# First score tiles in single PSUM banks, an earlier load of head 0, and re-paced weight sums in a two-layer decoder trunk

## The chip, the cores and the metric

The kernel runs on one core of one Trainium2 chip. The metric is the device time of one execution in microseconds; the median of several runs counts. The core has TensorE (PE), VectorE (DVE), ScalarE (ACT), GpSimd (POOL) and SyncE (SP); SP and POOL issue the DMAs here.

## What is computed

The reference is a decoder trunk of two layers on a sequence of 1024 tokens of width 1024, all in float32. Layer 0 is an mLSTM mixer and an MLP; layer 1 is causal attention with eight heads on low-rank keys and values, and an MLP. The hidden width of both MLPs is 4096, and the activation is the square of relu. Cut to what matters here:

```python
def causal_mla_attention(q_nope, q_rope, k_nope, k_rope, v):
    ...
    scale = (B_NOPE + B_ROPE) ** -0.5
    def block(args):
        qn_b, qr_b, start = args
        s = (jnp.einsum('bqhd,bkhd->bhqk', qn_b, k_nope)
             + jnp.einsum('bqhd,bkd->bhqk', qr_b, k_rope)).astype(jnp.float32) * scale
        ...
        s = jnp.where(kpos[None, :] <= qpos[:, None], s, -jnp.inf)
        p = jax.nn.softmax(s, axis=-1)
        return jnp.einsum('bhqk,bkhd->bqhd', p.astype(v.dtype), v)

def sqrelu_mlp(h, w1, w2):
    return jnp.square(jax.nn.relu(h @ w1)) @ w2
```

A query block is 128 tokens; the first one sees 128 keys, the last one 1024.

## The kernel before, in words

**Arithmetic.** Every float32 product is made of three passes with operands split into a high and a low part (`mm3`, L255 to L257): low times high, high times low, high times high. A split is a rounding copy on ACT and a subtraction on DVE (`split_mod`, L531 and L532; for weights L190 and L191, or L549 and L550 where the load and the split are traced apart by `wfetch`).

**Two halves and two streams.** The 1024 tokens are worked in two halves of 512. While one half runs its MLP (the dense stream), the other one's mixer runs in between. `two_streams` does the weaving by hand: the mixer is a generator that yields how many dense steps shall come next, or "align", which lets the dense stream run until its next step is one that makes a hidden tile. The first attention (`attention_first`) is that of tokens 0 to 511 and runs beside layer 0's MLP for tokens 512 to 1023; the second one (`attention_second`), tokens 512 to 1023, runs beside layer 1's MLP for tokens 0 to 511.

**PSUM.** The eight banks are handed out as two single banks `ps`, two single banks `pc` and two pairs of banks `pm`. The MLP makes a hidden tile in `ps` and its second product in `pm`; L199 adds that to the sum in SBUF. Transposes, the rotary product and some projections take `pc`. Attention scores take `pm`.

**One unit of attention.** A unit is one head with two query tiles, number 2j and 2j + 1. `scores` makes both (L1584 to L1590: four passes, on the diagonal block a fifth that adds the mask, and a last one; L1586 and L1587 read the rotary part T of the query) and calls `softmax` for each: maximum on DVE (L1594), scaling of it (L1595), Exp on ACT with the sum (L1596), reciprocal (L1597) and the product (L1598) on DVE, and for the even tile a zeroed block on POOL (L1600). `turned`, in `attend`, transposes the probabilities on PE (L1704) and splits them; `products` multiplies them with the values. For j = 0 one pair of banks holds the two tiles of a head, in one bank each, 128 and 256 keys wide (the matmul writes at least 256 columns). In the first attention the units of two heads go together, with j = 0 and 1; in the second a unit is one head, with j = 2 and 3.

**Preparing.** `prepare_pair` makes keys, values and queries of two heads for the present half. In the second half they go to DRAM (kd, vd, qd, td, 512 KB for each head and kind, td for two heads), and `loaded_head` brings a whole head back, keys and values of both halves: six loads for an even head. `query_rotary` (L1565 to L1570) makes T of the rotated query. All these tiles come from one ring of 24 buffers, `k4`.

**Weight sums.** The last MLP multiplies with sums of blocks of its first weight matrix. `weight_sums` makes them in DRAM with 128 DMAs from POOL, eight for each of 16 groups of rows, some of which add to what is there. Each one is handed out with a small DVE memset (L1046), a POOL copy of it (L1047) and the DMA (L1050 adds, L1052 writes). Of the eight, number 3 to 7 read or add to what the one before or an earlier one wrote. `with_weight_sums` hands out one per step of layer 0's MLP after its first 28 counted steps, and `with_rest` one per step of layer 1's MLP for tokens 0 to 511.

**Order.** The framework orders each engine's instructions before the run, by a priority and a simulated timeline. The priority is the order of tracing; `prompt(f)` traces what `f` makes 300 places ahead. Weight loads, their splits, the splits of hidden tiles and L199 are traced so already.

Of the kernel before, what the change touches and what calls it, by code (L numbers as in the profile page):

```python
# [83 lines left out]
def kernel(  # L84
# [66 lines left out]
    def pc():  # L151
        return pp.tile([P, 512], F32, tag="pc", bufs=2, name=f"pc_{next(uid)}")

    def pm():
        return pp.tile([P, 2, 512], F32, tag="pm", bufs=2, name=f"pm_{next(uid)}")
# [1406 lines left out]
    def query_rotary(qr):  # L1562
        T = k4v(F32R)
        hi = tmp(F32R)
        nc.scalar.copy(hi, qr)  # L1565

        nc.vector.tensor_copy(T[0:64, 0], hi[0:64].bitcast(F32))
        nc.vector.tensor_copy(T[64:128, 1], hi[64:128].bitcast(F32))
        nc.vector.tensor_sub(T[64:128, 0], qr[0:64], hi[0:64].bitcast(F32))
        nc.vector.tensor_sub(T[0:64, 1], qr[64:128], hi[64:128].bitcast(F32))  # L1570
        return T

# [19 lines left out]
    def softmax(f, pr, n, even):  # L1592
        m, l = small(1), small(1)
        nc.vector.reduce_max(m, f, axis=AX.X, negate=True)  # L1594
        nc.vector.tensor_scalar(m, m, SCALE, None, ALU.mult)  # L1595
        nc.scalar.activation(pr[:, :n], f, AF.Exp, bias=m, scale=SCALE, accum_out=l)  # L1596
        nc.vector.reciprocal(l, l)  # L1597
        nc.vector.tensor_scalar(pr[:, :n], pr[:, :n], l, None, ALU.mult)  # L1598
        if even:
            nc.gpsimd.memset(pr[:, n : n + P], 0.0)  # L1600

    def scores(kk, unit):

        (_, q, kn, _), j = unit
        prs = []
        if j < 2:
            st = pm()
            pr = raw().rearrange("p (a b) -> p a b", b=512)
            for e in range(2):
                score_mm(lambda g: st[:, e], kk, q, kn, 2 * j + e)  # L1610
            for e in range(2):
                n = (2 * j + e + 1) * P
                softmax(st[:, e, :n], pr[:, e], n, e == 0)
                prs.append(pr[:, e])
        else:
            for e in range(2):
                st = pm()
                n = (2 * j + e + 1) * P
                score_mm(lambda g: st[:, g], kk, q, kn, 2 * j + e)
                pr = raw()  # L1620
                softmax(st.rearrange("p a b -> p (a b)")[:, :n], pr, n, e == 0)
                prs.append(pr)
        return prs

# [6 lines left out]
    def prepare_pair(p_, hf):  # L1631


        wr, wkv = w_pair_r(p_), w_pair_kv(p_)
        yield 0
        wn, pt = w_pair_n(p_), pc()
        for k in range(3):
            mm3(pt, wr[0][:, k], wr[1][:, k], hf.cq[0][k], hf.cq[1][k], k == 0, k == 2)
        rp = rope(pt, hf)
        next(rp)  # L1640
        kt = [k4v(F32R) for _ in range(2)]
        kn = [(t[:, 0], t[:, 1]) for t in kt]
        k_half(kn, wkv, hf)
        for r in range(2):
            for i in range(2):
                nc.sync.dma_start(kd[2 * p_ + r, i, :, ts(hf.i, H)], kn[r][i].bitcast(F32))
        yield 1
        vt = [k4v(F32R, 256) for _ in range(2)]
        v = v_half(wkv, hf, vt)
        for r in range(2):  # L1650
            for i in range(2):
                nc.sync.dma_start(
                    vd[2 * p_ + r, i, :, ts(hf.i, H)].rearrange("p (t e) -> p t e", e=P),
                    vt[i][:, :, ts(r, P)].bitcast(F32),
                )
        qn = []
        for r in range(2):
            t = k4v(F32R)
            pt = pc() if r else ps()
            for k in range(3):  # L1660
                s = ts(r, P)
                mm3(pt, wn[0][:, k, s], wn[1][:, k, s], hf.cq[0][k], hf.cq[1][k], k == 0, k == 2)
            split_mod(t[:, 0], t[:, 1], pt, None)
            qn.append(t)
        T = query_rotary(last_of(rp))
        if hf.i:
            for r in range(2):
                nc.sync.dma_start(qd[2 * p_ + r], flat(qn[r]))
            nc.sync.dma_start(td[p_], flat(T))
            yield 1  # L1670
        else:
            yield 2
        vs = [[(h_[:, ts(r, P)], l_[:, ts(r, P)]) for h_, l_ in v] for r in range(2)]
        return [(2 * p_ + r, (qn[r], T[:, r]), kn[r], vs[r]) for r in range(2)]
# [18 lines left out]
    def attend(hf, groups, dense, behind=lambda: None):  # L1693


        def turned(work):
            PTh, PTl = hdv(F32R, 256), hdv(F32R, 256)
            n = 0
            for u, b0, nb in work:
                for b in range(b0, b0 + nb, 2):  # L1700
                    pt = pc()
                    for e in range(2):
                        for i in range(2):
                            nc.tensor.transpose(  # L1704
                                pt[:, ts(2 * e + i, P)], u.prs[i][:, ts(b + e, P)], ident
                            )
                    s = slice(n, n + 2)
                    split_mod(PTh[:, s], PTl[:, s], pt.rearrange("p (a b) -> p a b", b=256), None)
                    n += 2
            return PTh, PTl  # L1710

        def products(work, PT):
            n = 0
            for u, b0, nb in work:
                if b0 == 0:
                    u.po = ps()[:, :256]
                for kb in range(b0, b0 + nb):
                    mm3(u.po, *u.v[kb], PT[0][:, n], PT[1][:, n], kb == 0, kb == u.nk - 1)
                    n += 1
                if b0 + nb == u.nk:  # L1720
                    s = ts(u.j % 2, 256)
                    if u.hh < 6:
                        o = tmp()[:, :256]
                        nc.scalar.copy(o, u.po)
                        nc.sync.dma_start(oT[ts(u.hh, P), ts(u.j, 256)], o)
                    else:
                        split_mod(hf.o.hi[u.hh][:, s], hf.o.lo[u.hh][:, s], u.po, None)

        def begin():
            us = []  # L1730
            for head, j in next(groups, []):
                u = Half()
                (u.hh, _, _, u.v), u.j, u.nk = head, j, 2 * j + 2
                u.prs = scores(hf.kk, (head, j))
                us.append(u)
            return us

        late = None
        yield "align"
        us = begin()  # L1740
        yield 1
        while us:
            if sum(u.nk for u in us) <= 4:
                rounds = [[(u, 0, u.nk) for u in us]]
            else:
                rounds = [[(u, b, min(4, u.nk - b))] for u in us for b in range(0, u.nk, 4)]
            for n, work in enumerate(rounds):
                if late:
                    late()
                PT = turned(work)  # L1750
                late = lambda a=(work, PT): products(*a)
                if len(rounds) == 1:
                    yield 1
                if n == len(rounds) - 1:
                    us = begin()
                    if not us:
                        behind()
                yield next(dense)
        late()
# [15 lines left out]
    def attention_second(hf):  # L1775
        pairs = [prepare_pair(p_, hf) for p_ in range(4)]
        next(pairs[0])
        yield 0
        for p_ in range(4):
            if p_ < 3:  # L1780
                yield from primed(pairs[p_], pairs[p_ + 1])
            else:
                yield from pairs[p_]

        def units():
            for hh in range(NH):
                h_ = loaded_head(hh)
                if hh == 6:
                    last_o(hf)
                for j in range(2, 4):  # L1790
                    yield [(h_, j)]

        yield from attend(hf, units(), cycle((1, 0.5, 0.5)), lambda: load_o(hf))
# [365 lines left out]
    steps_done = [0]  # L2159

    def with_weight_sums(g):
        for v in g:
            if v != "within":
                steps_done[0] += 1
                if steps_done[0] > 28:
                    next(wsums, None)
            yield v

# [76 lines left out]
    def with_rest(g):  # L2245

        n = 0
        for v in g:
            if v != "within":
                n += 1  # L2250
                next(wsums, None)
                if n == 61:
                    later[0]()
            yield v
# [53 lines left out]
```

## Time and profile before

| | |
|---|---|
| median of 3 runs | 2362.25 us (2359.37 to 2362.75) |
| the profiled execution's own time | 2359.22 us |
| span in the profile, first to last instruction | 2357.3 us |
| granted clock of TensorE, mean | 0.997 |
| first attention, scores of the first pair to the last | 960.7 to 1199.8 us |
| second attention, first scores to the last | 1566.7 to 1813.1 us |
| DMA, mean rate | 178 GB/s |

In the timeline a row is: start in us, length in us, engine, line of the kernel, operation, the tiles it writes and reads, and the shape. Matmuls are pipelined: a 512-column one is shown with 0.39 us, and the next starts 0.23 us after it. In square brackets stands the idle time of the engine before it and what ended that. A row of the waits is: the waiting engine, tile and line, what it waited for, the total in us, how many times, the longest. A row of a stretch holds its bounds and length, the busy time of PE, PE's weight loads, DVE, ACT and POOL with their counts, the granted clock, the DMA engines' busy share and the rate in GB/s. A row of the chain that ended last is start, length and what it was.

### The profile page before, as it was taken

Reading aid. Unit: us, or ns where it says so; the run is one execution under the profiler, and the core shown is the slowest. Engines: PE = TensorE matmul, PEld = TensorE weight load, DVE = VectorE, ACT = ScalarE, POOL = GpSimd, SP = SyncE. Lnnn points to the kernel's source line nnn. Section 1 sums busy time; section 2 is a strip of 40 time slices with the busy share of each in tenths; the row PEclk is TensorE's granted clock in tenths of the full one; section 3 lists DMA queues with packets and bytes.
Section 4 is the critical chain, followed back from the end, with each engine's and each line's share of the span. In section 5 each row is a group of like instructions: output and inputs, shape, how many; then the busy total and the mean of one; then the engine's idle time right before and its main releaser. Section 6 shows DMA issues by size and latency. Waiting matters only on the chain.

```text
span 2357.3 us, 32527 instructions
## 1 busy us (share of the span) xinstructions
PE 2321.8 (98%) x12181; PEld 1959.9 (83%) x12181; DVE 1605.7 (68%) x2657; ACT 1098.2 (47%) x1826; POOL 155.0 (7%) x353
## 2 busy tenths in 40 slices
PE   7999999999999999999999999999999999999998
PEld 5888898888888888888888888888888888989997
DVE  6677876867685777777764967765656488557556
ACT  4355335654343354334444554434444445655543
POOL 1010000000001110111010110010001000000000
PEclk9999999999999999999999999999999999999999
DMA  9452664545566876667764665885544553656562
GB/s 314 144 153 82 191 184 149 156 141 163 174 184 179 284 222 188 184 195 207 211 160 126 199 200 183 274 274 172 163 134 134 143 164 97 185 173 217 166 185 88
DMA packets 408349, 420.76 MB, mean 178 GB/s; under 512 B 27427, under 2 KB 310112, under 8 KB 404608
## 3 DMA queue, kind: packets, MB, share of 16 engines
q1 hardware_dynamic: 402272, 385.02, 52.1%
q0 software_dynamic: 5920, 33.66, 6.5%
q8 instruction: 96, 1.57, 0.3%
q14 instruction: 61, 0.50, 0.1%
HBM read 359.37 MB, written 92.80 MB: 192 GB/s over the span
## 4 chain that ended last, share of the span: by engine, by line
PE 89%; DVE 5%; DMA 4%; ACT 1%; issue 1%; SPq 0%; DVEq 0%; ACTq 0%
PE ps L255 15%; PE ps L257 15%; PE ps L256 15%; PE pm L255 10%; PE pm L256 10%; PE pm L257 10%; DMA raw<-in_mlp_w_dram 2%; PE pc L256 2%; PE pc L257 2%; PE pc L255 2%; PE pc L1704 1%; DMA raw<-in_a_w_in_dram 1%; PE pm L1590 1%; PE pm L899 1%; PE pm L1584 1%
## 5 line engine op out<-in xcount | busy, mean ns | idle before, releaser
L255 PE MATMUL ps<-k,wl 128*128 128x512 f32 (+1 forms) x1432 | 546.3, 381 | 1.6 <-DVE wl L191 1.3
L257 PE MATMUL ps<-k,wh 128*128 128x512 f32 (+1 forms) x1432 | 539.0, 376 | 0.0
L256 PE MATMUL ps<-k,wh 128*128 128x512 f32 (+1 forms) x1432 | 537.4, 375 | 0.0
L549 ACT CAST wh<-raw 128x1024 fp32r<-128x1024 f32 x272 | 285.0, 1051 | 481.4 <-PE ps L255 149.0
L550 DVE TENSOR_TENSOR wl<-raw,wh 128x1024 fp32r<-128x1024 f32 x272 | 331.7, 1221 | 249.4 <-ACT wh L549 155.4
L255 PEld LDWEIGHTS ps<-k,wl 128*128 128x128 f32 x1432 | 269.6, 188 | 53.7 <-issue 3.6
L257 PEld LDWEIGHTS ps<-k,wh 128*128 128x128 f32 x1432 | 269.4, 188 | 50.1 <-issue 0.7
L256 PEld LDWEIGHTS ps<-k,wh 128*128 128x128 f32 x1432 | 269.8, 188 | 48.9 <-issue 1.7
L199 DVE TENSOR_TENSOR k<-k,pm 128x512 f32<-128x512 f32 (+1 forms) x254 | 210.9, 858 | 83.3 <-PE pm L257 82.0
L191 DVE TENSOR_TENSOR wl<-raw,wh 128x1024 fp32r<-128x1024 f32 (+2 forms) x110 | 128.1, 1166 | 115.6 <-ACT wh L190 115.4
L255 PE MATMUL pm<-hd,wl 128*128 128x512 f32 x512 | 201.4, 393 | 0.5 <-ACT hd L531 0.5
L256 PE MATMUL pm<-hd,wh 128*128 128x512 f32 x512 | 199.3, 390 | 0.2 <-DVE hd L532 0.2
L257 PE MATMUL pm<-hd,wh 128*128 128x512 f32 x512 | 199.3, 390 | 0.0
L255 PE MATMUL pm<-wh,hd 128*128 128x512 f32 x488 | 192.2, 394 | 2.9 <-ACT raw L1596 2.5
L256 PE MATMUL pm<-wl,hd 128*128 128x512 f32 x488 | 190.3, 390 | 0.0
L257 PE MATMUL pm<-wh,hd 128*128 128x512 f32 x488 | 190.2, 390 | 0.0
L190 ACT CAST wh<-raw 128x1024 fp32r<-128x1024 f32 (+2 forms) x110 | 109.4, 996 | 172.3 <-PE ps L255 82.9
L1596 ACT ACTIVATE raw<-pm,sm 128x128 f32<-128x128 f32 (+3 forms) x64 | 47.5, 742 | 152.4 <-DVE sm L1595 122.8
L532 DVE TENSOR_TENSOR hd<-tmp,hd 128x512 fp32r<-128x512 f32 x128 | 88.0, 688 | 38.6 <-ACT hd L531 37.9
L255 PEld LDWEIGHTS pm<-hd,wl 128*128 128x128 f32 x512 | 96.2, 188 | 21.0 <-ACT hd L531 0.9
L256 PEld LDWEIGHTS pm<-hd,wh 128*128 128x128 f32 x512 | 96.2, 188 | 20.5 <-DVE hd L532 0.5
L257 PEld LDWEIGHTS pm<-hd,wh 128*128 128x128 f32 x512 | 96.1, 188 | 20.1
(391 smaller groups left out, 4274.9 us busy)
## 6 DMA issues: line engine op xcount, KB each, us to landing
raw<-in_mlp_w_dram SPq DMA_DIRECT2D x240, 512.0 KB, 4.3
raw<-in_ada_w_dram SPq DMA_DIRECT2D x80, 512.0 KB, 4.6
raw<-in_a_w_in_dram SPq DMA_DIRECT2D x48, 512.0 KB, 4.4
sums<-in_mlp_w_dram POOLq DMA_DIRECT2D x96, 256.0 KB, 4.5
raw<-sums SPq DMA_DIRECT2D x64, 256.0 KB, 3.7
xs<-k SPq DMA_DIRECT2D x40, 256.0 KB, 5.6
raw<-in_kv_ada_w_dram SPq DMA_DIRECT2D x16, 512.0 KB, 4.1
raw<-in_a_w_out_dram SPq DMA_DIRECT2D x16, 512.0 KB, 4.9
```

Source lines behind the costliest of these rows:

```text
L190: nc.scalar.copy(hi[:, :n], r[:, :n])
L191: i = nc.vector.tensor_sub(lo[:, :n], r[:, :n], hi[:, :n].bitcast(F32))
L199: return f(*a, **k)
L255: nc.tensor.matmul(o, ll, rh, start=start, stop=False, **m)
L256: nc.tensor.matmul(o, lh, rl, start=False, stop=False, **m)
L257: pe_last[0] = nc.tensor.matmul(o, lh, rh, start=False, stop=stop, **m)
L532: nc.vector.tensor_sub(lo, u, hi.bitcast(F32))
L549: nc.scalar.copy(hi, u)
L550: nc.vector.tensor_sub(lo, u, hi.bitcast(F32))
L899: nc.tensor.matmul(nv[:, r, i], hf.PT[p_][:, r, cs], v[2 * p_ + r], start=g == 0, stop=True,)
L1584: nc.tensor.matmul(o[:, :w], ql, kh, start=True, stop=False)
L1596: nc.scalar.activation(pr[:, :n], f, AF.Exp, bias=m, scale=SCALE, accum_out=l)
```

## The change

- `scores`: for j = 0 a head's two tiles take one `pc` bank, 256 columns each, where they took a `pm` pair. The j = 1 tiles and the second attention keep `pm`.
- `softmax`, the split of transposed probabilities in `turned`, and `query_rotary` are wrapped in `prompt`.
- `prepare_pair` of the second half loads head 0 (`hf.first`) before it stores the queries and T of the last pair; `units` takes that head in place of loading it itself.
- `with_weight_sums` starts after 44 counted steps, where it started after 28. `with_rest` hands out one operation per step for the first 11 steps, none for steps 12 to 22, and two per step from step 23 on.

```diff
         if j < 2:
-            st = pm()
+            st = pm() if j else pc().rearrange("p (a b) -> p a b", b=256)
             pr = raw().rearrange("p (a b) -> p a b", b=512)
...
                 n = (2 * j + e + 1) * P
-                softmax(st[:, e, :n], pr[:, e], n, e == 0)
+                prompt(softmax)(st[:, e, :n], pr[:, e], n, e == 0)
                 prs.append(pr[:, e])
...
-                softmax(st.rearrange("p a b -> p (a b)")[:, :n], pr, n, e == 0)
+                prompt(softmax)(st.rearrange("p a b -> p (a b)")[:, :n], pr, n, e == 0)
...
-        T = query_rotary(last_of(rp))
+        T = prompt(query_rotary)(last_of(rp))
         if hf.i:
+            if p_ == 3:
+                hf.first = loaded_head(0)
             for r in range(2):
                 nc.sync.dma_start(qd[2 * p_ + r], flat(qn[r]))
             nc.sync.dma_start(td[p_], flat(T))
...
                     s = slice(n, n + 2)
-                    split_mod(PTh[:, s], PTl[:, s], pt.rearrange("p (a b) -> p a b", b=256), None)
+                    prompt(split_mod)(
+                        PTh[:, s], PTl[:, s], pt.rearrange("p (a b) -> p a b", b=256), None
+                    )
...
             for hh in range(NH):
-                h_ = loaded_head(hh)
+                h_ = loaded_head(hh) if hh else hf.first
...
                 steps_done[0] += 1
-                if steps_done[0] > 28:
+                if steps_done[0] > 44:
                     next(wsums, None)
             yield v
...
                 n += 1
-                next(wsums, None)
+                for _ in range(1 if n < 12 else 0 if n < 23 else 2):
+                    next(wsums, None)
                 if n == 61:
                     later[0]()
```

## The prediction

> **What bounds the kernel now.** I read the page first: the share of each engine, then the chain that ended last.
>
> ```profile
> span 2357.3 us, 32527 instructions
> PE 2321.8 (98%) x12181; PEld 1959.9 (83%) x12181; DVE 1605.7 (68%) x2657; ACT 1098.2 (47%) x1826; POOL 155.0 (7%) x353
> PE 89%; DVE 5%; DMA 4%; ACT 1%; issue 1%; SPq 0%; DVEq 0%; ACTq 0%
> ```
>
> PE is busy for 98% of the span and 89% of the chain is its own work. The change leaves PE's work as it is (the same matmuls, to other banks), so all it can win is time that PE waits, and whatever wait goes anywhere moves the end by as much. The next view is therefore PE's waits in the stretches that the diff touches: the first attention (945 to 1220 us), then the second one in two parts.
>
> ```profile
> PE pm L1584 <- DVE k L199: 2.9, 4, 0.9
> PE pm L1584 <- DVE sm L1046: 1.2, 3, 0.5
> PE pm L255 <- ACT raw L1596: 1.9, 2, 1.1
> PE pm L1586 <- DMA k<-td: 1.1, 1, 1.1
> PE pm L255 <- ACT raw L1596: 0.6, 2, 0.4
> PE pc L1704 <- DVE raw L1598: 0.5, 3, 0.2
> ```
>
> The first two rows are the first attention, the next two 1500 to 1620 us, the last two 1620 to 1830 us: 4.1, 3.0 and 1.1 us of idle PE. They understate the loss, because a row ends where a matmul's modelled end lies. The timeline of one place shows by how much, with DVE and ACT beside it:
>
> ```profile
> 960.01 0.39 PE L257 MATMUL pm<-hd,wh 128*128 128x512 f32 x1
> 960.75 0.39 PE L1584 MATMUL pm<-k,k 128*128 128x256 f32 x1 [0.35 <-DVE sm L1046]
> 961.36 0.37 PE L1590 MATMUL pm<-k,k 128*128 128x256 f32 x1
> 961.57 0.27 PE L1584 MATMUL pm<-k,k 128*128 128x256 f32 x1
> 962.07 0.36 PE L1590 MATMUL pm<-k,k 128*128 128x256 f32 x1
> 963.15 0.38 PE L1584 MATMUL pm<-k,k 128*128 128x256 f32 x1 [0.71 <-DVE k L199]
> 970.18 1.03 PE L1704 MATMUL pc<-ident,raw 128*128 128x128 f32 x8
> 958.75 0.69 DVE L1570 TENSOR_TENSOR k<-tmc,tmp 64x512 fp32r<-64x512 f32 x1
> 959.47 1.22 DVE L199 TENSOR_TENSOR k<-k,pm 128x1024 f32<-128x1024 f32 x1
> 961.88 1.21 DVE L199 TENSOR_TENSOR k<-k,pm 128x1024 f32<-128x1024 f32 x1
> 963.68 0.28 DVE L1594 TENSOR_REDUCE sm<-pm 128x1 f32<-128x128 f32 x1
> 964.83 0.40 DVE L1594 TENSOR_REDUCE sm<-pm 128x1 f32<-128x256 f32 x1
> 968.22 0.37 DVE L1598 TENSOR_SCALAR raw<-raw,sm 128x256 f32<-128x256 f32 x1
> 964.26 0.37 ACT L1596 ACTIVATE raw<-pm,sm 128x128 f32<-128x128 f32 x1 [5.31 <-DVE sm L1595]
> ```
>
> The scores of the first head start 0.74 us after the last MLP matmul, where the next 512-column one starts after about 0.23; the second head's start 1.08 after the last of the first, where 961.36 to 961.57 shows 0.21 for the same seam. So 0.51 and 0.87 us are lost where the rows say 0.35 and 0.71: 0.16 more per wait. The reason stands on DVE: both bank pairs (pm) still hold the MLP's products, and the two additions that empty them (L199) end at 960.69 and 963.09, each just before a score starts. (The row that names a memset, L1046, names what lay beside the first of them.)
>
> **Scores in pc banks.** For j = 0 each head takes one 512-column pc bank instead of a pm pair; its two 256-column tiles fit. The four pairs of heads have 7 such waits: 4.1 + 7 x 0.16 = 5.2 us, and up to 6.0 if the slower first matmul behind each wait (about 0.11) goes too. Are the pc banks free? Their last users are the query's evacuation and the rotary product; the latter is read before L1570 can start at 958.75, 1.5 us before the scores are due. What is late next is the rotary query that the third matmul of a score reads: L1570 ends at 959.44, and that matmul would come at about 960.6, so it holds by 1.1 us. After that come the transposes (L1704), which need the softmax. Without the waits (0.51 + 0.87 + 2 x 0.11) the scores end 1.6 us earlier and the transposes are due at 970.18 - 1.6 = 968.6; the softmax of the four tiles on DVE now ends at 968.59 behind the additions. If DVE keeps its order, that is even, with perhaps 0.1 us lost a place; if the softmax, now marked urgent, passes the second addition or the work between the two, nothing. I take 5.2 - 4 x 0.05 = 5.0 us gained; the bounds are 2.0 (each place slips by 0.75) and 6.0.
>
> Sharing a bank has a price of its own: the second tile's maximum may have to wait for the first tile's Exp. In the rows above, in two different banks, it does so already: ACT's Exp ends at 964.63 and the second maximum starts at 964.83. The Trainium skill, PSUM — Partial Sum Buffer, section "PSUM bank collisions raise a hardware error", says that two engines may not touch one bank in the same quadrant at once, reads included, which speaks against this edit. By that rule the first maximum would also wait for the second tile's six matmuls, 0.6 to 0.7 us by their rows, and with four places this part would be 5.0 - 2.6 = 2.4 us. I don't take it, since DVE is busy with the addition until 963.09 anyway, long after those matmuls.
>
> **The early load of head 0.** The second attention's first score waits for the td tile:
>
> ```profile
> 1555.33 3.45 SPq L1668 DMA_DIRECT2D qd<-k  x2
> 1558.83 1.26 SPq L1681 DMA_DIRECT2D k<-kd  x2
> 1566.90 0.39 PE L1585 MATMUL pm<-k,k 128*128 128x512 f32 x1
> 1568.39 0.50 PE L1586 MATMUL pm<-hd,k 128*128 128x512 f32 x1 [1.10 <-DMA k<-td]
> 1560.71 7.64 DMA k<-td
> ```
>
> From 1566.90 to 1568.39 is 1.49 us where 0.23 is due: 1.26 lost. Six loads (two kd, qd, td, two vd) move past two qd stores and one td store on SP's queue; the second qd store keeps SP until 1558.78. Ahead of the stores the loads issue up to 3.5 us earlier, so td lands near 1564.9, 2 us before it is read. The stores come about 6 x 0.4 = 2.5 us later, and only the tiles that they free wait for them. The loads need six k4 tiles while 24 are handed out (8 for the MLP's input, 4 for its sum, 2 + 3 latents, 7 of the last pair); seven of these are done with by then (two stored keys, the latents). I take 1.2 gained, bounds 0 (the loads find no tile and wait) and 1.4.
>
> **Softmax, turned splits and rotary query marked urgent.** No instruction is added; the fixed order on DVE, ACT and POOL changes, and what gets passed is the splits of weights and hidden tiles, which the MLP needs a step or two later. The waits after 1620 us are 1.1 + 5 x 0.27 = 2.4 us (0.16 and 0.11 more for each, as above); most are the length of the softmax itself, which no order shortens. I take 0.3, bounds -0.5 (a late weight split) and 2.4.
>
> **Weight sums.** 128 operations are handed out one per MLP step, and the last starts at 1822.6:
>
> ```profile
> L1046 DVE MEMSET sm<- x128: 59/59/59, 695.5 to 1822.6; 128x1 f32 x128
> 695.00:840.00 145.00, 145.00 (x644) 119.25 (x643) 94.58 (x159) 57.94 (x76) 24.64 (x52) 1.00 0.76 228
> 1500.00:1620.00 120.00, 116.84 (x593) 98.41 (x592) 77.04 (x129) 47.89 (x76) 10.49 (x26) 1.00 0.80 249
> 1620.00:1825.00 205.00, 203.34 (x1155) 174.00 (x1154) 127.80 (x234) 90.29 (x157) 19.84 (x50) 1.00 0.48 147
> q0 software_dynamic: 480, 2.88, 11.6%
> q0 software_dynamic: 736, 4.46, 9.8%
> POOL sums L1050 <- DMA sums<-sums: 26.4, 6, 6.2
> 1974.38 0.92 SPq L236 DMA_DIRECT2D raw<-sums  x2
> ```
>
> By the code 24 + 64 steps hand them out before the second layer, and 40 steps of it the rest; after it is 8 + 64, then 11, none for 11 steps, then 45 in 23 steps: it ends five steps later, near 1855, over 100 us before the first read at 1974.38. Where they go, early on (695 to 840), PE is busy throughout: nothing gained. The 11 silent steps are the stretch from 1500 to 1620, where DMA is at 0.80, of which the sums (q0) are 11.6%. There a weight load takes 8.58 us and is the cause of the two waits in the 1.9 us row above:
>
> ```profile
> 1591.20 8.58 DMA raw<-in_mlp_w_dram
> 1592.63 0.52 POOL L1052 DMA_DIRECT2D sums<-sums  x1
> ```
>
> It lands at 1591.20 + 8.58 = 1599.8, and DVE stands behind its split (L550) with the softmax queued behind that. One 256 KB sum that starts 1.4 us after the load will be gone; the loads of heads beside it stay. Of 1.9 + 2 x 0.27 = 2.4 us I take 1.0, bounds 0 and 2.4.
>
> **The sum.** 5.0 + 1.2 + 0.3 + 1.0 = 7.5 us, by the bounds 1.5 to 12.2. The profiled execution took 2359.22 us (span 2357.3 and 1.9 around it), 3.0 under the median of 2362.25; it would come to 2351.7, and the median to 2354.75, say 2354.8. A measurement of this kernel tells about 0.2%, 4.7 us, from no change.
>
> **Rivals.** (1) Given back: the waits before scores go, but the transposes wait for the softmax (0.75 us at four places) and td or the late load stays: 2.0 + 0.9 = about 3 us, median 2359. For it: DVE's softmax end and the due time of the transposes are even. Against: the urgent mark. (2) Slower: from 1620 on two sums per step make the weight loads late. Behind a late load DVE stands as at 1600, which costs PE 2.4 us each time. Of the 16 units of scores (eight heads, two each) twelve come after 1620; with half of them so struck it is 6 x 2.4 = 14 us against 7.5: median 2369. It decides once DMA there comes near the 0.80 of the stretch that has the late load. The sums (q0) now take 9.8% there; 18 operations become about 35, so the share goes from 0.48 to about 0.58: not near on the mean, though in bursts. By the Trainium skill, DMA: Bandwidth & Descriptors, section "Issuing engines are not separate DMA queues", transfers of POOL and SP run on the same 16 engines and interleave; the two stretches above, 0.80 with a late load and 0.48 with none, agree. POOL's own queue is no cover either: of a step's two operations, one in four pairs reads what its partner writes, and POOL then stands up to 6.2 us, the zeroing for the softmax (L1600) behind it. That gets read about 10 us later, as these rows show, so PE sees none of it unless two such waits follow each other:
>
> ```profile
> 1610.94 0.20 POOL L1600 MEMSET raw<- 128x128 f32 x1 [0.57 <-issue]
> 1621.09 0.60 PE L1704 MATMUL pc<-ident,raw 128*128 128x128 f32 x4
> ```
>
> (3) It doesn't do what it says: the scores keep waiting, now for a pc bank, or the order stays; 0 to 1 us, median 2362.
>
> **How the numbers follow.** Forecast 0.57, (1) 0.24, (3) 0.06, (2) 0.13. Only the forecast is faster by over 0.2%; (1) and (3) are within it, less a little that turns slower by a reshuffled order: faster 0.57, same 0.29, slower 0.14. The low end is the sum of upper bounds with a microsecond for the median's scatter, 2362.25 - 12.2 - 1 = 2349; the high end takes in (1) and (3) and the scatter of the three runs, 2363.5, and leaves (2) out.
>
> **What would show it.** Right: no wait of L1584 on L199 in the first attention; L1584 writes pc there 16 times; L1704 waits under 1 us there; no wait on td; no sums DMA between about 1500 and 1620 and twice the count after it; PE's idle time about 5 us less. Wrong: L1704 waiting on L1598 or POOL for over 3 us; waits of L255 on L1596 growing after 1620 with weight loads that take over 8 us; a wait of the scores for pc.

## The result and the profile after

The changed kernel takes 2374.67 us (median of 5 runs, 2373.26 to 2378.23), the kernel before, run beside it, 2362.25 (5 runs, 2358.35 to 2363.58). The ratio is 1.0057 [1.0043, 1.0070], 13.5 us slower (10.2 to 16.5), where 7.5 us faster was forecast. The profiled execution took 2375.45 us, 16.2 more than that of before. From here on "expected" and "measured" times are medians, and positions in us are those of one profiled execution each.

The same three rows of the page, then PE's waits in the same stretches (shifted by 15 us where the kernel is late) and one stretch more, the end of layer 0's first MLP, 690 to 850 us:

```profile
span 2373.8 us, 32557 instructions
PE 2326.8 (98%) x12181; PEld 1965.2 (83%) x12181; DVE 1607.2 (68%) x2657; ACT 1098.0 (46%) x1826; POOL 156.2 (7%) x353
PE 89%; DVE 4%; DMA 4%; ACT 1%; issue 1%; SPq 0%; DVEq 0%; ACTq 0%
```

```profile
PE ps L255 <- DVE wl L550: 6.3, 1, 6.3
PE pm L255 <- DVE wl L550: 4.3, 1, 4.3
...
PE ps L256 <- DVE hd L532: 1.4, 2, 0.8
...
PE pm L255 <- ACT raw L1596: 1.1, 1, 1.1
PE pm L1586 <- DMA k<-td: 0.5, 1, 0.5
...
PE pm L255 <- ACT raw L1596: 3.9, 4, 3.2
```

The page hardly shows it: the shares are those of before. The waits do. The first two rows are 690 to 850 us, where the kernel before has no wait of PE at all: 10.6 us behind the splits of two weight tiles. The next one is the first attention: the waits of the scores (4.1 us before) are gone, and 1.4 us stand behind a hidden split. Then 1500 to 1620 (place of before), where td cost 1.1 and now costs 0.5, and 1620 to 1830, where one wait of 3.2 us for a softmax is new.

Lined up by the same matmul in both traces, the changed kernel is 0.7 us late at 525 us, 15.7 late at 804 us, 12.5 late at the end of the first attention, 12.0 at 1647 us, and 16.2 after the wait at 1716 us. So 15.0 us are lost in the first MLP, 3.2 won up to the end of the first attention, 0.5 in the second one, and 4.2 lost again there. The 3.2 are 4.2 won from the first scores on, less 1.1 lost just ahead of them, between 840 and 950 us.

Here is the first loss, DVE and ACT in the kernel before (start, length, engine, line, what):

```profile
747.69 0.28 DVE L1414 TENSOR_REDUCE lbias<-pc 128x1 f32<-128x128 f32 x1
747.89 0.28 DVE L1403 TENSOR_SCALAR tma<-raw,kvada 128x128 f32<-128x128 f32 x1
750.91 1.22 DVE L1408 TENSOR_TENSOR raw<-raw,mods 128x1024 f32<-128x1024 f32 x1
...
753.32 1.03 ACT L190 CAST wh<-raw 128x1024 fp32r<-128x1024 f32 x1
754.78 2.00 ACT L549 CAST wh<-raw 128x1024 fp32r<-128x1024 f32 x2
```

And the same work in the changed kernel, with PE:

```profile
748.35 0.28 DVE L1414 TENSOR_REDUCE lbias<-pc 128x1 f32<-128x128 f32 x1
754.74 0.69 DVE L532 TENSOR_TENSOR hd<-tmp,hd 128x512 fp32r<-128x512 f32 x1 [6.11 <-ACT hd L531]
755.35 0.28 DVE L1403 TENSOR_SCALAR tma<-raw,kvada 128x128 f32<-128x128 f32 x1
759.75 1.22 DVE L1408 TENSOR_TENSOR raw<-raw,mods 128x1024 f32<-128x1024 f32 x1
763.23 1.22 DVE L550 TENSOR_TENSOR wl<-raw,wh 128x1024 fp32r<-128x1024 f32 x1
...
761.01 1.04 ACT L190 CAST wh<-raw 128x1024 fp32r<-128x1024 f32 x1 [6.30 <-DVE raw L1408]
761.96 2.93 ACT L549 CAST wh<-raw 128x1024 fp32r<-128x1024 f32 x3
...
764.50 0.80 PE L255 MATMUL ps<-k,wl 128*128 128x512 f32 x1 [6.30 <-DVE wl L550]
765.09 0.63 PE L256 MATMUL ps<-k,wh 128*128 128x512 f32 x1
```

L1403 to L1408 are background work: `latent_weights` scales a block of weights for the attention, long before it is needed. Before, the block follows L1414 at once. After, it stands behind the low part of a hidden split (L532), and DVE idles for 6.11 us until ACT has made that split's high part. The block ends 8.8 us later in the trace. ACT waits for it 6.30 us, because the block's own split (L190) is ahead of three weight splits (L549) in ACT's queue. DVE makes the low parts after that (L550), and PE has run out of weights. At 778 to 787 us the same happens with the next block, 4.3 us.

Nothing in this stretch was edited but the start of the weight sums. What ties them to the block are two lines of the kernel that the prediction did not follow:

```python
    def paced():
        return tc.issue_after(pace[0]) if pace[0] else nullcontext()
...
                pace[0] = next(i for i in reversed(traced) if i.engine == dve)
```

Background work on DVE is ordered behind a mark, the last DVE instruction that was traced in the MLP's step. In the kernel before, from step 29 on, that is the memset of a weight sum (L1046), which waits for next to nothing (all 128 of them kept DVE idle for 0.8 us). In the changed kernel steps 29 to 44 have no sum, and the mark is the step's own last instruction, here the hidden split. This is **theory M (the mark)**. Its rivals: the sums' transfers or instructions do it in another way (T), or the attention edits shift the order there (A). For the second loss the prediction's own rival (2) is at hand: **R2**, two sums per step make a weight load late. Against it stands G, that the eleven silent steps do it.

### The profile page after: what moved, and what is told of

It is laid out like the page before. It is cut to its first block, busy times and chain, and to the rows that moved or that the text cites. A ratio compares the mean times of both kernels' runs of the same rounds, so it can differ in the third digit from the quotient of the medians.

```text
span 2373.8 us, 32557 instructions
## 1 busy us (share of the span) xinstructions
PE 2326.8 (98%) x12181; PEld 1965.2 (83%) x12181; DVE 1607.2 (68%) x2657; ACT 1098.0 (46%) x1826; POOL 156.2 (7%) x353
## 4 chain that ended last, share of the span: by engine, by line
PE 89%; DVE 4%; DMA 4%; ACT 1%; issue 1%; SPq 0%; DVEq 0%; ACTq 0%
PE ps L255 15%; PE ps L256 15%; PE ps L257 15%; PE pm L255 10%; PE pm L256 10%; PE pm L257 10%; PE pc L255 2%; PE pc L257 2%; PE pc L256 2%; PE pc L1706 1%; DMA raw<-in_a_w_in_dram 1%; DMA raw<-in_mlp_w_dram 1%; PE pm L1590 1%; DVE sm L1594 1%; PE pm L1586 1%
## 5 line engine op out<-in xcount | busy, mean ns | idle before, releaser
L549 ACT CAST wh<-raw 128x1024 fp32r<-128x1024 f32 x272 | 284.7, 1050 | 478.7 <-PE ps L255 148.0
L550 DVE TENSOR_TENSOR wl<-raw,wh 128x1024 fp32r<-128x1024 f32 x272 | 332.1, 1223 | 250.6 <-ACT wh L549 160.7
L190 ACT CAST wh<-raw 128x1024 fp32r<-128x1024 f32 (+2 forms) x110 | 109.3, 996 | 182.2 <-PE ps L255 81.4
L532 DVE TENSOR_TENSOR hd<-tmp,hd 128x512 fp32r<-128x512 f32 x128 | 88.2, 690 | 47.8 <-ACT hd L531 47.2
L255 PEld LDWEIGHTS pm<-wh,hd 128*128 128x128 f32 x488 | 92.1, 189 | 25.3 <-ACT raw L1596 7.0
```

Source lines behind the costliest of these rows:

```text
L190: nc.scalar.copy(hi[:, :n], r[:, :n])
L255: nc.tensor.matmul(o, ll, rh, start=start, stop=False, **m)
L532: nc.vector.tensor_sub(lo, u, hi.bitcast(F32))
L549: nc.scalar.copy(hi, u)
L550: nc.vector.tensor_sub(lo, u, hi.bitcast(F32))
```

## The experiments

All times are medians, with the ratio to the kernel before, measured beside it, and its 95% interval. The ratio is estimated from all the runs and need not be the quotient of two medians; where us are given for a ratio, they are its share of the kernel before.

| kernel | us | ratio |
|---|---|---|
| changed kernel | 2374.67 | 1.0057 [1.0043, 1.0070] |
| before, sums start after 44 | 2372.54 | 1.0060 [1.0046, 1.0073] |
| changed, sums start after 28 | 2361.18 | 1.0003 [0.9994, 1.0012] |
| changed, bare memset in steps 29 to 44 | 2361.56 | 1.0005 [0.9996, 1.0014] |
| before, memset not the mark up to 44 | 2376.59 | 1.0069 [1.0055, 1.0084] |
| before + the attention edits | 2355.54 | 0.9981 [0.9972, 0.9990] |
| before + pc banks | 2356.75 | 0.9980 [0.9971, 0.9989] |
| before + urgent marks | 2361.83 | 0.9997 [0.9987, 1.0007] |
| before + early head 0 | 2359.48 | 0.9997 [0.9986, 1.0008] |
| before + layer 1's re-paced sums | 2366.39 | 1.0020 [1.0011, 1.0029] |
| attention edits + gap, one per step | 2356.35 | 0.9975 [0.9965, 0.9985] |
| the same + an empty second | 2356.26 | 0.9980 [0.9972, 0.9989] |
| attention edits + marks from step 1 | 2353.51 | 0.9966 [0.9954, 0.9979] |

**The start of the sums, alone.** On the kernel before:

```diff
-                if steps_done[0] > 28:
+                if steps_done[0] > 44:
```

> The kernel before with one line changed: the weight sums start after step 44 instead of 28; nothing of the attention is touched. Theory M: all of the loss of the first MLP is there, two waits of PE for L550 between 760 and 795 us, about 2362.3 + 15 = 2377 us (2375 to 2379), above the changed kernel since none of the attention's gain is in it. Rival A (it is the attention edits): 2362. Rival R2 (two per step later): one per step stays here, so 2362.

Measured 1.0060, that is 14.2 us (10.9 to 17.2), with both waits for L550 (6.3 and 4.3 us). The median itself, 2372.54, lies under the expected 2375 to 2379; the kernel before ran at 2360.58 beside it, where 2362.3 was counted on. Rivals A and R2 fall for this stretch: no attention edit is in this kernel, and it has one sum per step.

**The start put back.** In the changed kernel, the reverse of that line.

> The changed kernel with one line put back: the weight sums start after step 28 again. Theory M (the mark): up to step 44 the sums' memset was the last VectorE instruction of each MLP step, and so the mark behind which the background work (the latent blocks of L1403 to L1408) is placed; without it the mark is the step's own last instruction, which waits for the MLP, and the background work falls late. By it the two waits of the first MLP (6.3 us of PE for the split L550 at 764.5, 4.3 at 787.5) go and with them some 15 us: about 2374.7 - 15 = 2359.7 us, between 2358 and 2362. Rival R2 (two sums per step after 1620 us make weight loads late): the first MLP is not the cause that lasts; the sums now end earlier, so less than 4 us comes back there and the rest stays at about 2370. Rival A (the attention edits shift the order of the first MLP too): nothing comes back in 690 to 830 us, 2374.

Measured 1.0003, 2361.18 us: 13 us come back. The time is 1.5 us above theory M's middle value and within its range. What is left against the kernel with the attention edits alone (0.9981) is 0.0022, 5.2 us; see below.

**A bare mark.** In the changed kernel, nothing but a memset in the steps that lost their sums:

```diff
                 if steps_done[0] > 44:
                     next(wsums, None)
+                elif steps_done[0] > 28:
+                    with paced():
+                        nc.vector.memset(small(1), 0.0)
```

> The changed kernel, where steps 29 to 44 get one paced memset of a one-column tile on VectorE and nothing else: no DMA and no GpSimd instruction comes back, and the sums themselves start after step 44 as in the changed kernel. Theory M: the memset alone is the mark, so the loss of the first MLP goes as in the run that starts at 28: 2359.7 us (2358 to 2362), within 1 us of that run but for what the sums' later end costs. Rival T (it is the sums' traffic or their instructions that shifted something, or the removed work had kept the clock or the queues in step): a bare memset brings nothing back, 2374.

Measured 1.0005, as with the start put back. Its DVE rows, and its row of the stretch 695 to 840 us (start and end, length, busy time of PE, PE's loads, DVE, ACT, POOL with counts, clock, DMA share, GB/s):

```profile
748.15 0.28 DVE L1414 TENSOR_REDUCE lbias<-pc 128x1 f32<-128x128 f32 x1
748.35 0.28 DVE L1403 TENSOR_SCALAR tma<-raw,kvada 128x128 f32<-128x128 f32 x1
```

```profile
695.00:840.00 145.00, 145.00 (x644) 119.25 (x643) 95.26 (x159) 57.72 (x75) 9.14 (x20) 1.00 0.64 199
```

The block follows L1414 again and PE is busy throughout, though POOL has 9.14 us of work there instead of the 24.64 of the kernel before, and the DMA share is 0.64 instead of 0.76. So neither the transfers nor the copies matter there; T falls in that form.

**The mark taken away, all else left.** On the kernel before, the sums stay at all their steps; the memset is only passed over when the mark is chosen, up to step 44 (`unmarked` starts as an empty set):

```diff
-                    nc.vector.memset(flag, 0.0)
+                    m = nc.vector.memset(flag, 0.0)
+                    if steps_done[0] <= 44:
+                        unmarked.add(m.ins.name)
...
-                pace[0] = next(i for i in reversed(traced) if i.engine == dve)
+                pace[0] = next(
+                    i for i in reversed(traced)
+                    if i.engine == dve and i.name not in unmarked
+                )
```

> The kernel before, all weight sums at their old steps with their memsets, copies and DMAs; the one change is that for the first 44 counted steps the memset does not count as the mark of its step, so that the step's own last VectorE instruction does. Theory M (the mark): the loss of the first MLP is there although no operation was taken away, two waits of PE for the split L550 between 760 and 795 us, about 2360.6 + 12 to 15 = 2373 to 2376 us, like the run that starts after 44. Rival (the memset matters because it or its DMA takes time or a place, not as a mark): 2360.6, no such wait.

Measured 1.0069, 16.3 us (13.0 to 19.8). The median, 2376.59, is 0.6 us over the expected range; in the trace 15.7 us are lost from 525 to 804 us (15.0 in the changed kernel), and 2.8 more at a longer wait for td. Its waits of PE from 690 to 850 us, and its DVE (lines shifted by 1 to 3):

```profile
PE ps L256 <- DVE wl L551: 6.3, 1, 6.3
PE pm L256 <- DVE sm L1047: 4.3, 1, 4.3
```

```profile
748.47 0.28 DVE L1417 TENSOR_REDUCE lbias<-pc 128x1 f32<-128x128 f32 x1
754.86 0.69 DVE L533 TENSOR_TENSOR hd<-tmp,hd 128x512 fp32r<-128x512 f32 x1 [6.11 <-ACT hd L532]
755.47 0.28 DVE L1406 TENSOR_SCALAR tma<-raw,kvada 128x128 f32<-128x128 f32 x1
```

The same two waits to the tenth, with the same work as before (the second row names a memset that lay beside the split). Theory M is shown from both sides: a mark without the sums cures it, the sums without the mark have it.

**The attention edits alone** (bank per head, urgent marks, early head 0; the sums as before).

> The attention edits alone on the kernel before (bank per head for the first scores, the three urgent marks, the early load of head 0); the sums as before. By the landmarks of the changed kernel's trace the first attention gave back 3.2 us and the second one about 0.5 before a late load at 1715 us took 4.1. If that late load belongs to two sums per step (R2), it is not here: 2362.3 - 3.5 = 2358.8 us, between 2357 and 2360. If it belongs to the attention edits (the early load of head 0 shifts the later loads), it is here too: 2362.

Measured 0.9981, 4.5 us gained (2.4 to 6.6). The median, 2355.54, is 1.5 us under the expected range, beside a kernel before that ran 1.7 us faster than was counted on. No wait for the softmax is longer than 0.5 us after 1620: the 3.2 us wait belongs to the sums. Each edit alone, first the banks:

> The kernel before with the first scores in single pc banks and nothing else; no urgent marks, no early head. The three attention edits together give 5.0 us (2360.6 to 2355.5). By the prediction's step the banks alone give 5.0 of it, bounds 2.0 and 6.0: 2355.6. Rival (the transposes then wait for the softmax, which is not urgent here): about 3, 2357.6.

0.9980, 4.7 us (2.6 to 6.8): the prediction's 5.0 is in it, the rival's 3 as well. The rival's mechanism falls, as the transposes (L1704) do not wait in the first attention. Its size can't be told from 5.0: in the trace the first attention gives 5.7 us, but against a trace of before whose scores wait 4.1 us there, the most of six traces with the old banks; the others have 2.1 to 3.2. Then the marks and the early head:

> The kernel before with the three urgent marks (softmax, turned split, rotary query) and nothing else. The three attention edits together gave 5.1 us and the banks alone 4.5, so 0.6 is left for the marks and the early head. By the prediction's step the marks give 0.3, bounds -0.5 and 2.4: about 2360.9, no difference from the kernel before that can be told. Rival (they let the scores or the transposes come earlier by themselves): 2 us or more, under 2359.2.

> The kernel before with head 0 of the second attention loaded ahead of the last stores and nothing else. By the prediction's step the wait for td goes: 1.2 us, bounds 0 and 1.4, so 2360.0. In the traces with all three attention edits the row of that wait fell only from 1.1 to 0.5 us, so 0.5 is as likely: 2360.7. Rival (later loads are shifted against each other): 2362 or more.

Both 0.9997, which can't be told from nothing. In the trace of the early head alone the wait for td falls from 1.1 to 0.2 us, so the mechanism is there at 0.9 us. The other traces agree: 0.2 to 0.5 us wherever head 0 is loaded early, 0.7 to 1.9 where it isn't. The marks alone have, in the first attention, a wait of 0.8 us of PE for the hidden split (L532) that the kernel before does not have:

```profile
PE pm L1584 <- DVE k L199: 1.6, 2, 0.9
PE ps L256 <- DVE hd L532: 0.8, 1, 0.8
```

It is the row that the changed kernel has with 1.4 us. The banks alone have it with 0.2.

**Two sums per step.** Layer 1's re-pacing alone on the kernel before:

```diff
-                next(wsums, None)
+                for _ in range(1 if n < 12 else 0 if n < 23 else 2):
+                    next(wsums, None)
```

> The kernel before with the re-paced sums of layer 1 alone: one per step, eleven silent steps, then two per step; the start stays at 28, the attention is not touched. Theory R2 (traffic of two sums beside one weight load): the loss of 5.6 us that stood beside the attention edits is here too, one wait of PE for the Exp of L1596 of about 3 to 4 us near 1715: 2361.2 + 5 = 2366, less 1 if the silent steps take the late load at 1600 away. Rival (it needs the earlier head loads of the attention edits beside it): 2361.

Measured 1.0020, 4.7 us lost (2.6 to 6.8), with a wait of 3.3 us near 1703 us. So the attention edits are not needed for it. Then, on the attention edits, the gap without the doubling, and the gap with the second sum's memset and copy but no DMA for it:

```diff
-                next(wsums, None)
+                if not 12 <= n < 23:
+                    next(wsums, None)
+                if n >= 23:
+                    flag, seen = small(1), small(1)
+                    with paced():
+                        nc.vector.memset(flag, 0.0)
+                    nc.gpsimd.tensor_copy(seen, flag)
```

The first of the two has only the first two added lines.

> The attention edits alone, with the eleven silent steps of the re-paced sums but one sum per step afterwards. The run with two per step cost 5.6 us more than the attention edits alone, nearly all of it at about 1700 us. Theory R2 (two per step make the weight load late): with one per step that loss is gone, 2355.5 us (2354 to 2357), or up to 1 us better since the gap frees the stretch 1500 to 1620. Rival G (it is the gap, which shifts the order and the phase of the sums against the loads): 2361.

> The same with the gap and one sum per step afterwards, and in place of the second sum of a step its memset on VectorE and its copy on GpSimd without a DMA. Tells the traffic of the second sum from its place in the order of VectorE and GpSimd. If the transfers are what makes the load late: as with one sum per step, about 2355.5. If it is the second memset and copy (a later mark, GpSimd's queue): about 2361, as with two sums per step.

0.9975 and 0.9980, both as good as the attention edits alone: G falls, and so does the second memset as a cause. What is left is the second transfer. One weight load shows how, first with the attention edits alone, then with two sums per step (changed kernel, start put back), in the chain of waits; below each the sums that POOL issues beside it:

```profile
1682.74 8.08 DMA raw<-in_mlp_w_dram
1690.85 1.05 ACT wh L549
1691.93 1.22 DVE wl L550
```

```profile
1683.85 0.52 POOL L1052 DMA_DIRECT2D sums<-sums  x1
```

```profile
1684.39 10.69 DMA raw<-in_mlp_w_dram
1695.10 1.05 ACT wh L549
1697.32 0.82 DVE sm L1594
1698.89 0.89 ACT raw L1596 x2
1699.83 0.65 PE pm L255
```

```profile
1685.03 1.22 POOL L1050 DMA_DIRECT2D sums<-in_mlp_w_dram  x1 [0.27 <-issue]
1686.16 0.72 POOL L1052 DMA_DIRECT2D sums<-in_mlp_w_dram  x1
```

DVE stands behind the late tile's low part (L550), the maximum of the softmax (L1594) is next on DVE, and PE waits 3.9 us for its Exp, where it waited 0.5 before. Against the matmuls the load lands 3.7 us later: 2.6 are its length, and 1.1 its later start, most of it behind two head loads that SP takes 0.76 us longer to issue. The same load takes 8.05 us in the kernel before and 8.34 and 8.89 in the last two kernels, all with one sum beside it. It takes 10.07 with the re-pacing alone, 10.51 in the changed kernel and 11.40 with the bare mark, all with two. The Trainium skill, DMA: Bandwidth & Descriptors, section "Issuing engines are not separate DMA queues", says that SP's and POOL's transfers share the engines; these durations agree.

**Marks from step 1 on.** The attention edits, the sums as before, and a bare paced memset in steps 1 to 28 too:

> The three attention edits, sums as before, and a paced memset as the mark in the first 28 counted steps too, where no sum runs yet. If a mark that waits for nothing is better wherever background work runs beside an MLP, the steps up to 690 us lose a little of what PE waits: 2355.5 less up to 1 us. If the background work is not late there, as PE's row of waits has no split of a weight before 690 us, the same: 2355.5. Rival (background work then runs ahead of the MLP's own splits): slower, 2357 or more.

0.9966 [0.9954, 0.9979]: the best median, 2.0 us under the 2355.5 of which up to 1 us was expected to go, but its interval overlaps that of the attention edits alone (0.9972 to 0.9990). In its trace nothing is gained before 690 us (1.5 us behind the kernel before at 525 and at 804 us alike), so a gain by the marks is not shown.

## Why the prediction was wrong

**The failed step** is the one on the weight sums: "Where they go, early on (695 to 840), PE is busy throughout: nothing gained." It asked what the removed operations cost while they were there and found 59 ns of DVE each, off the path. It did not ask what else hangs on them. The memset was also the mark behind which DVE's background work is placed, so taking it away was worth 14.2 us the wrong way (10.9 to 17.2, the start alone). No bound and no rival held this. The row that could have raised the question stood in the prediction: L1046 counted 128 times, one per step, in the very stretch where `latent_weights` runs under `paced()`.

**The terms.** Banks: 5.0 forecast, 4.7 measured. There is no wait of the scores left, L1584 writes pc 16 times (the first row below), and the transposes do not wait in the first attention. So the mechanism was right. The size fits, in part by luck: it was worked out from the 4.1 us of one trace, the longest such wait of six. A slip was in the cover: the softmax passed neither the second addition nor the work behind it (L383), as the rows of DVE in the changed kernel show (the addition ends at 979.36, the first maximum starts at 979.94):

```profile
L1584 PE MATMUL pc<-k,k x16: 273/280/284, 977.0 to 1194.7; 128*128 128x256 f32 x16
978.15 1.21 DVE L199 TENSOR_TENSOR k<-k,pm 128x1024 f32<-128x1024 f32 x1
979.28 0.74 DVE L383 SCALAR_TENSOR_TENSOR tma<-raw,cond,tma 128x512 f32<-128x512 f32 x1
979.94 0.28 DVE L1594 TENSOR_REDUCE sm<-pc 128x1 f32<-128x128 f32 x1
```

It cost nothing: PE has no wait for the softmax in the first attention.

Early head: 1.2 forecast, 0.9 in its trace, not to be told by time; with the other edits 0.5 of td's 1.1 stays in the changed kernel. Urgent marks: 0.3 forecast, nothing that can be told. They put up to 0.8 us at a time on a hidden split, the kind of cost that the prediction had as its lower bound, -0.5. That they take waits off the scores is not shown: 2.2 us are left there with the marks alone, within the 2.1 to 4.1 of the old banks without them. Layer 1's sums: 1.0 forecast, 4.7 lost. The wait near 1600 us, which the silent steps were to take away, is 1.1 us in the changed kernel where it was 1.9; with the attention edits alone, sums as before, it is 1.1 too, so not even that part is shown to be theirs.

**Rival (2) was right in mechanism** and wrong in size: six places at 2.4 us, where one place at 4 to 5 us came. The DMA share from 1635 to 1840 us is 0.57 against the 0.58 it worked out, and it decided below the 0.80 that it had set as its point: a burst did it. The prediction called the stretch after 1620 us one with no late load, and that reading was wrong: in the kernel before, the load at 1688 us takes 8.05 us and already costs PE 0.4 us, the longest wait in its own row for that stretch. So this load had no slack, and what made it longer went to PE. Why the other long loads after 1620 us cost PE 0.7 us at most together was not tried. The last sum is handed out at 1907.9 us, not near 1855, still ahead of its first read at 1990.9: the five more steps take some 69 us, where 32 were counted.

**The sum, made again**: 0.9981 (attention) x 1.0060 (start) x 1.0020 (two per step) = 1.0061, inside the measured 1.0043 to 1.0070. So the three parts hardly touch each other. Of the forecast's 7.5 us the attention's 6.5 came to 4.5; the change lost all of it and more in the two edits of the weight sums, one of which was forecast at nothing.

## What to carry to other kernels

Before an instruction is costed at nothing and removed, look for what is ordered by it: where the order is planned from marks, "the last instruction of the step" changes its meaning when the last instruction goes. A mark should be something that waits for nothing; here a 59 ns memset in the right place was worth 13 us. Traffic that is moved to where DMA has room on the mean has to be laid beside the single load that PE's next split waits for, not beside the mean.

## What the runs showed of the hardware

A long wait of PE costs more than its length. After the three longest waits of the changed kernel, 512-column matmuls came every 427 ns instead of every 227 for some microseconds. The stretches show the granted clock (the third column from the right, ahead of DMA share and rate), first in the changed kernel, then in the kernel without the mark, at its wait for td:

```profile
757.00:764.00 7.00, 1.19 (x6) 0.65 (x4) 5.51 (x8) 2.99 (x4) 0.00 (x0) 0.83 0.16 65
764.00:768.00 4.00, 3.50 (x8) 2.82 (x9) 2.71 (x3) 0.89 (x1) 0.00 (x0) 0.50 1.11 272
787.00:792.00 5.00, 4.48 (x11) 3.55 (x12) 2.70 (x4) 1.62 (x2) 0.00 (x0) 0.50 0.98 286
1715.70:1717.20 1.50, 1.41 (x6) 1.20 (x7) 1.46 (x4) 0.04 (x1) 0.00 (x0) 1.00 0.00 0
1717.20:1720.60 3.40, 3.40 (x10) 2.67 (x9) 1.13 (x4) 2.82 (x4) 0.00 (x0) 0.51 0.00 0
```

```profile
1582.60:1584.60 2.00, 0.06 (x1) 0.00 (x0) 0.48 (x1) 0.00 (x0) 0.00 (x0) 1.00 0.95 373
1586.50:1588.50 2.00, 2.00 (x7) 1.66 (x7) 0.98 (x2) 0.23 (x1) 0.00 (x0) 0.50 1.02 418
```

After the waits of 6.30 and 4.32 us the clock is at half from the first matmul on; after one of 3.22 us it falls some 1.5 us after work resumed. The slow matmuls (8, 10 and 8 of them, 0.2 us too late each) add 1.6, 2.0 and 1.6 us to the three waits. So 6.30 + 4.32 + 1.6 + 2.0 and twice 0.16, which the rows understate, make 14.5 of the 15.0 us lost in the first MLP. The Trainium skill, TensorE: Matmul & The Clock Gate, section "HAM oscillation — how this bites in real kernels", gives the rule that PE should not idle for more than about 3.4 us. Here a wait of 3.22 us and one of 1.94 us (with one of 0.20 us just ahead of it) were followed by the half clock too, and the 1.1 us waits of the kernel before were not. The 14 traces give no sharp limit. Leaving out the first 50 us and the end of the kernel, each of the eleven waits of 1.94 us or more had a half clock, which began in the wait or up to 1.5 us after it. Of the waits of 1.0 to 1.9 us three had one, all near 267 us (1.24, 1.38 and 1.39 us: banks alone, start put back, marks alone), while others up to 1.86 us had none. No half clock stands elsewhere.
